# Sums of the first four steps' up weights by accumulating transfers, and the turned input's differences on VectorE

## The chip, the cores and the metric

The kernel runs on one core of a Trainium2 chip. A core has five engines that run beside each other, each with its own queue in program order: TensorE (PE, matrix products), VectorE (DVE), ScalarE (ACT), GpSimd (POOL), and SyncE (SP), which here only issues transfers. Transfers between HBM and the on-chip memory run on 16 DMA engines. The metric is the device time of one execution in microseconds (us); the median of several runs is compared.

## The reference, cut to what matters

The reference is one decoder block over 1024 tokens of width 1024. Its last part is the one that matters here, with 5632 hidden columns of which one half is a value and the other a gate:

```python
def conv_ffn(x, w_up, conv_w, conv_b, w_down):
    h = x @ w_up
    h = causal_depthwise_conv(h, conv_w) + conv_b      # width 3
    a, g = jnp.split(h, 2, axis=-1)
    return (jax.nn.silu(g) * a) @ w_down

h = h + mix @ w_out
h = h + conv_ffn(rmsnorm(h, norm_ffn_g), w_up, conv_w, conv_b, w_down)
return rmsnorm(h, norm_final_g)
```

## The kernel before, in words

**Matrix products.** Float32 operands are taken apart into a high part (a rounded copy, made by ScalarE, L153) and a low part (the rest, by VectorE, L159: `low = source - high`), and three matmuls make one float32 product: high by high, high by low, low by high. So VectorE has one instruction of 128x512 for every weight block. Large products use Winograd's form of the two-by-two block product: seven block products in place of eight, with sums of weight blocks (S1 to S4) and sums of input blocks (T1 to T4) as operands. One block product here is 12 matmuls of 128x512 (function `product`, L1015).

**The passage around the change.** After the eight attention heads the output projection runs over eight blocks of 128 tokens in the order 0, 4, 1, 5, 2, 3, 6, 7 (`wmm`, `hadd`, `norm2`). Each block's result is normed and turned by eight transposes on TensorE (`flip`, L957). For the upper four token blocks `flip` also forms the differences of the turned input: VectorE computes `b11 - p`, `t3`, `t2` (L977 to L979), the high and low parts of T2 and T3 follow (L951, L954), and GpSimd computes `b21 = t2 - b21` (L982). When the last block (7) is turned, `late_sum` (L1044) makes the parts of T1, T4 and B22.

**The up stage** has 22 steps, i = 0 to 21, one for each pair of 128 value columns and 128 gate columns. Step i needs four weight blocks A11, A12 (one load of 512 KB, `upw_a`, L882) and A21, A22 (another, `upw_b`, L898), and the four sums

S1 = A21 + A22, S2 = S1 + A11, S3 = A21 + A11, S4 = S2 + A12,

which GpSimd adds (L907 to L910) into four tiles "sg" of 128x512, a ring of four. In step 1 alone (`inplace`, L902 to L904 and L910) three of the sums are written over the raw blocks, since the ring is taken by step 0. Weights of steps 0 and 1 (AHEAD = 2) are loaded and summed during the last head and the projection; those of step i + 1, from step 2 on, during step i (`nxt_of`, L1141, a generator that `up_b` advances at four places). Raw blocks lie in a ring of four 512 KB tiles "raw"; the parts of A11 and A12 in a ring of four ("wha"), those of S1, S2, S3, S4 and A22 in one of six ("whb"). `product` runs in the order A11, S2, S3, A12, S1, A22, S4 within a step, with the next step's first matmuls drawn ahead.

`up_b` (L1075) puts together the results in VectorE's instructions L1082 to L1105, runs the convolution (L1069 on ScalarE, L1070 and L1072 on VectorE) for gate and value, Silu on ScalarE, and stores the hidden columns and their sums (L1119 to L1124). One order is written out by hand: the low parts of A11 and A12 of steps 2 and 3 stand on VectorE's queue behind the lower gate half of the step before (`gates["hg"]`, L1094). The rest of the order on each queue is a scheduler's; the tile pools put the waits in.

Of the kernel before, what the change touches and what calls it, by code (L numbers as in the profile page):

```python
# [12 lines left out]
ALU = mybir.AluOpType  # L13
# [51 lines left out]
def block_kernel(ctx: ExitStack, tc: tile.TileContext, xT, xtok, wuv, wv, wqk, wf, cpk, bfv,  # L65
                 ggain, g2r, gfr, wsp, woa, wos, wup, wdn, out):
    nc = tc.nc
    act, dve, pool, pe, sp = Line(nc.scalar, tc), Line(nc.vector, tc), Line(nc.gpsimd, tc), nc.tensor, nc.sync
# [22 lines left out]
    def sb(tag, shape, dt=F32):  # L91
        return (raws if tag == "raw" else late if tag in LATE else early).tile(shape, dt, tag=tag, bufs=BUFS[tag], name=nm(tag))
# [7 lines left out]
    def sbank():  # L100
        return psa.tile([P, 512], F32, tag="s", name=nm("ps"))
# [48 lines left out]
    def split_w(src, hl, hi_eng="act", lo_eng="dve"):  # L150
        h, l = hl
        if hi_eng == "act":
            act.copy(h, src)  # L153
        elif hi_eng == "pool":
            pool.tensor_copy(h, src)
        else:
            dve.tensor_copy(h, src)
        eng = dve if lo_eng == "dve" else pool
        return eng.tensor_tensor(out=l, in0=src, in1=f32(h), op=ALU.subtract)  # L159
# [3 lines left out]
    def behind(inst, key):  # L163

        if key in gates:
            after(tc, inst, gates[key])
# [30 lines left out]
    def ring(dt=F32R):  # L197
        rn[0] += 1
        return sb(RTAG[(rn[0] - 1) % 6], [P, 2, 512], dt)
# [10 lines left out]
    def hl_of(n, j, src):  # L210
        act.copy(x2(n, 0, j), src)
        dve.tensor_tensor(out=x2(n, 1, j), in0=src, in1=f32(x2(n, 0, j)), op=ALU.subtract)
# [19 lines left out]
    for p_ in range(2):  # L232
        t = sb("G", [P, 2, 2, 512])
# [100 lines left out]
    for j in range(2):  # L334
        t1, t2, t3 = tmp[j]
# [29 lines left out]
    for j in range(2):  # L365
        t2 = tmp[j][1]
# [66 lines left out]
    W = [Weights(0)]  # L433
# [177 lines left out]
    for k in range(4):  # L611
        t = sb("raw", [P, 2, 512])
# [9 lines left out]
    for hf in (1, 0):  # L622
        for c in range(4):
            src = vgt[hf][:, :, c * P:(c + 1) * P].rearrange("p t (g d) -> p g t d", g=2)
# [17 lines left out]
    for p_ in range(2):  # L642
        t = ring(F32)
# [228 lines left out]
    def ut_(pool_, tag, shape, dt, bufs):  # L872
        return pool_.tile(shape, dt, tag=tag, bufs=bufs, name=nm(tag))
# [3 lines left out]
    AHEAD = 2  # L877
# [13 lines left out]

        return out, split

    def upw_b(i, out, inplace=False):

        a11, a12 = out["ra"][:, 0, :], out["ra"][:, 1, :]
        wr = sb("raw", [P, 2, 512])
        sp.dma_start(out=wr, in_=wup[i, :, 0:2, :])  # L898
        a21, a22 = wr[:, 0, :], wr[:, 1, :]
        if inplace:  # L900
            s = [a21, ut_(upl, "sg", [P, 512], F32, 4), a11, a12]
            pool.tensor_tensor(out=a11, in0=a21, in1=a11, op=ALU.add)  # L902
            pool.tensor_tensor(out=s[1], in0=a11, in1=a22, op=ALU.add)
            pool.tensor_tensor(out=a21, in0=a21, in1=a22, op=ALU.add)  # L904
        else:
            s = [ut_(upl, "sg", [P, 512], F32, 4) for _ in range(4)]
            pool.tensor_tensor(out=s[0], in0=a21, in1=a22, op=ALU.add)  # L907
            pool.tensor_tensor(out=s[1], in0=s[0], in1=a11, op=ALU.add)  # L908
            pool.tensor_tensor(out=s[2], in0=a21, in1=a11, op=ALU.add)
        pool.tensor_tensor(out=s[3], in0=s[1], in1=a12, op=ALU.add)  # L910
        src = {"A22": a22, "S1": s[0], "S2": s[1], "S3": s[2], "S4": s[3]}

        def split(names):
            for n in names:
                t = ut_(upr, "whb", [P, 2, 512], F32R, 6)
                behind(split_w(src[n], (t[:, 0], t[:, 1])), "sums")
                out[n] = t
            return out

        return split  # L920
# [36 lines left out]
    def flip(tt):  # L957

        c = slice((tt % 4) * P, (tt % 4) * P + P)
        pp = []  # L960
        for kh in range(2):
            ps = sbank()
            for j in range(4):
                k = 4 * kh + j
                pe.transpose(ps[:, j * P:(j + 1) * P], xn[tt][:, k * P:(k + 1) * P], ident)
            pp.append(ps.rearrange("p (k t) -> p k t", k=4))
        if tt < 4:
            for n, p3 in (("B11", pp[0]), ("B21", pp[1])):
                hl_of(n, c, p3)
            for n, p3 in (("B11", pp[0]), ("B21", pp[1])):  # L970
                act.copy(xt[n][:, :, c], p3)
            return
        b11, b21, b22 = (xt[n][:, :, c] for n in ("B11", "B21", "B22"))
        t3 = ut_(xtp, "t3", [P, 4, P], F32, 1)
        t2 = ut_(xtp, "t2", [P, 4, P], F32, 1)
        act.copy(b22, pp[1])
        dve.tensor_tensor(out=b11, in0=b11, in1=pp[0], op=ALU.subtract)  # L977
        dve.tensor_tensor(out=t3, in0=b22, in1=pp[0], op=ALU.subtract)
        d = dve.tensor_tensor(out=t2, in0=b22, in1=b11, op=ALU.add)  # L979
        hl_of("T2", c, t2)  # L980
        hl_of("T3", c, t3)
        pool.tensor_tensor(out=b21, in0=t2, in1=b21, op=ALU.subtract)  # L982
        return d

    WA = [upw_a(i) for i in range(AHEAD)]
    W = [WA[0][1](("A11", "A12"))]
    first = (0, 4, 1, 5)
    banks8 = {(tt, hf): (bank() if hf == 0 else sbank()) for tt in first for hf in range(2)}
    for tt in first:
        for hf in range(2):  # L990
            wmm(tt, hf, banks8[tt, hf], (0, 1, 2))
    W.append(WA[1][1](("A11", "A12")))
    WB = [upw_b(0, W[0]), upw_b(1, W[1], True)]
    prev = None
    for tt in (0, 4, 1, 5, 2, 3, 6, 7):
        hload(tt)
        for hf in range(2):
            if tt in first:
                wmm(tt, hf, banks8[tt, hf], (3,))
                hadd(tt, hf, banks8[tt, hf])  # L1000
            else:
                ps = bank()
                wmm(tt, hf, ps, range(4))
                hadd(tt, hf, ps)
        norm2(tt)
        if prev is not None:
            flip(prev)
        prev = tt
# [20 lines left out]
    for i in range(AHEAD):  # L1029
        for j in range(2):  # L1030
            q = psq("a")
            product(q, W[i]["A11" if j == 0 else "A12"], XB["B11" if j == 0 else "B21"], True, True)
            ahead.append(q)
        if i == 0:

            last = flip(7)
            WB[0](("S2", "S3"))
            gates["sums"] = last

    def late_sum(n, src):  # L1040
        for j in range(2):
            k = slice(2 * j, 2 * j + 2)
            act.copy(XB[n][:, 0, k, :], xt[src][:, k, :])
            dve.tensor_tensor(out=XB[n][:, 1, k, :], in0=xt[src][:, k, :], in1=f32(XB[n][:, 0, k, :]), op=ALU.subtract)  # L1044

    late_sum("T1", "B11")
    WB[0](("S1",))
    late_sum("T4", "B21")
# [81 lines left out]
    def waited(i):  # L1130

        x1 = ut_(pst_[0], "u", [P, 512], F32, 5)
        ha = ut_(pst_[0], "h", [P, 1024], F32, 3)
        act.copy(x1, ahead[2 * i])
        dve.tensor_tensor(out=ha[:, 0:512], in0=ahead[2 * i + 1], in1=x1, op=ALU.add)
        return None, x1, ha

    st = waited(0)
    WB[0](("A22", "S4"))

    def nxt_of(i):  # L1141

        if i + 1 == NFF:
            while True:
                yield None
        if i + 1 < AHEAD:
            w, wb = W[i + 1], WB[i + 1]
            wa = lambda names: None
        else:
            w, wa = upw_a(i + 1)  # L1150
            wb = upw_b(i + 1, w)
            W.append(w)
        yield None
        wa(("A11",))
        wb(("S2",))
        yield waited(i + 1) if i + 1 < AHEAD else up_a(i + 1, w)
        wa(("A12",))
        wb(("S3",))
        yield None
        wb(("S1", "A22", "S4"))  # L1160
        yield None
# [21 lines left out]
    for p_, n in ((upl, "B11"), (upl, "T2"), (upl, "B21"), (upl, "T3"), (upr, "T1"), (upr, "T4"), (upr, "B22")):  # L1183
        t = ut_(p_, "x" + n, [P, 2, 4, 512], F32, 1)
# [37 lines left out]
    def blk(b):  # L1222
        return lambda p_: wd[p_][:, b, :]
# [129 lines left out]
```

## Time and profile before

| | |
|---|---|
| median of 3 runs | 1100.56 us (1096.5 to 1100.8) |
| the profiled execution, its own time | 1103.27 us |
| its span in the trace | 1101.5 us |
| granted TensorE clock, mean | 0.991 |
| TensorE busy | 1073.1 us |
| VectorE busy | 900.0 us |
| ScalarE busy | 572.7 us |
| GpSimd busy | 249.2 us |

Times in the rows are microseconds from the span's start. A row of the timeline has the start, the duration, the engine, the line, the operation and its tiles, how often it follows itself, and in brackets how long the engine was idle before it and which instruction released it. Durations overlap the next instruction's start a little, so the distance between starts is the better price of an instruction in a dense row. Windows give the busy time of each engine in a stretch with the number of instructions, and then the granted clock, the busy share of the DMA engines and their GB/s. The matmuls of the up stage's twenty-two steps lie between 452.0 and 884.8 us.

### The profile page before, as it was taken

Reading aid. Unit: us, or ns where it says so; the run is one execution under the profiler, and the core shown is the slowest. Engines: PE = TensorE matmul, PEld = TensorE weight load, DVE = VectorE, ACT = ScalarE, POOL = GpSimd, SP = SyncE. Lnnn points to the kernel's source line nnn. Section 1 sums busy time; section 2 is a strip of 40 time slices with the busy share of each in tenths; the row PEclk is TensorE's granted clock in tenths of the full one; section 3 lists DMA queues with packets and bytes.
Section 4 is the critical chain, followed back from the end, with each engine's and each line's share of the span. In section 5 each row is a group of like instructions: output and inputs, shape, how many; then the busy total and the mean of one; then the engine's idle time right before and its main releaser. Section 6 shows DMA issues by size and latency. Waiting matters only on the chain.

```text
span 1101.5 us, 14438 instructions
## 1 busy us (share of the span) xinstructions
PE 1073.1 (97%) x5013; PEld 881.8 (80%) x5013; DVE 900.0 (82%) x1355; ACT 572.7 (52%) x991; POOL 249.2 (23%) x205
## 2 busy tenths in 40 slices
PE   9999999999998999988999999999999999999997
PEld 6888787777887888766888888888888888888886
DVE  5985799775678977999798989999998876898774
ACT  6656544454468865653444444444444454454653
POOL 0002243133035331334232423333232000000000
PEclk9999999899999999999999999999999999999999
DMA  9242366846548345113123232313321899433342
GB/s 339 85 153 78 100 169 181 231 140 209 189 133 268 98 144 188 70 67 134 68 105 134 78 114 96 124 68 123 116 96 45 270 330 324 122 97 101 124 137 96
DMA packets 64714, 158.18 MB, mean 144 GB/s; under 512 B 7673, under 2 KB 7937, under 8 KB 64641
## 3 DMA queue, kind: packets, MB, share of 16 engines
q1 hardware_dynamic: 64352, 156.70, 42.5%
q8 instruction: 39, 0.64, 0.2%
q10 hardware_dynamic: 288, 0.56, 0.1%
q14 instruction: 35, 0.28, 0.1%
HBM read 114.95 MB, written 42.27 MB: 143 GB/s over the span
## 4 chain that ended last, share of the span: by engine, by line
PE 67%; DVE 7%; ACT 3%; DMA 2%; issue 2%; POOL 1%; SPq 0%; DVEq 0%; ACTq 0%; POOLq 0%
PE k L1210 18%; PE qd L1020 10%; PE qa L1020 10%; PE qc L1020 9%; PE qb L1020 5%; PE pb L794 2%; PE ps L256 2%; PE pb L784 2%; PE pf L824 1%; PE pf L823 1%; PE pf L825 1%; DVE whb L159 1%; DMA rsd<-t 1%; PE ps L759 1%; PE ps L758 1%
## 5 line engine op out<-in xcount | busy, mean ns | idle before, releaser
L1210 PE MATMUL k<-whb,wha 128*128 128x512 f32 x924 | 209.6, 389 | 0.0
L1210 PEld LDWEIGHTS k<-whb,wha 128*128 128x128 f32 x924 | 173.4, 188 | 36.1
L1020 PE MATMUL qa<-xB,wha 128*128 128x512 f32 x528 | 129.4, 395 | 5.7 <-DVE wha L159 5.7
L1020 PE MATMUL qc<-xT,whb 128*128 128x512 f32 x540 | 130.3, 390 | 1.7 <-DVE xT L951 1.3
L1020 PEld LDWEIGHTS qa<-xB,wha 128*128 128x128 f32 x528 | 100.2, 190 | 27.3 <-DVE wha L159 6.5
L1020 PEld LDWEIGHTS qc<-xT,whb 128*128 128x128 f32 x540 | 101.1, 188 | 23.8 <-DVE xT L951 1.8
L153 ACT CAST wha<-sg 128x512 fp32r<-128x512 f32 x77 | 47.9, 622 | 97.3 <-PE k L1210 87.1
L153 ACT CAST whb<-sg 128x512 fp32r<-128x512 f32 x85 | 52.0, 616 | 70.3 <-PE qc L1020 67.7
L159 DVE TENSOR_TENSOR wha<-sg,wha 128x512 fp32r<-128x512 f32 x77 | 52.9, 689 | 42.5 <-ACT wha L153 42.4
L159 DVE TENSOR_TENSOR whb<-sg,whb 128x512 fp32r<-128x512 f32 x85 | 63.0, 742 | 8.9 <-ACT whb L153 8.7
L1020 PE MATMUL qd<-xB,whb 128*128 128x512 f32 x264 | 64.6, 393 | 0.1
L794 PE MATMUL pb<-pt,V 128*128 128x256 f32 (+1 forms) x320 | 60.1, 301 | 4.6 <-ACT pt L785 4.0
L1020 PE MATMUL qd<-xT,whb 128*128 128x512 f32 x264 | 63.4, 389 | 0.0
L1020 PE MATMUL qb<-xT,whb 128*128 128x512 f32 x252 | 61.0, 389 | 1.0 <-DVE whb L159 1.0
L794 PEld LDWEIGHTS pb<-pt,V 128*128 128x128 f32 x320 | 48.0, 192 | 16.6 <-ACT pt L785 11.4
L785 ACT CAST pt<-pb 128x512 fp32r<-128x512 f32 (+1 forms) x80 | 41.0, 543 | 36.7 <-PE pb L784 36.0
L786 DVE TENSOR_TENSOR pt<-pb,pt 128x512 fp32r<-128x512 f32 (+1 forms) x80 | 48.6, 634 | 13.3 <-ACT pt L785 12.8
L1020 PEld LDWEIGHTS qd<-xB,whb 128*128 128x128 f32 x264 | 50.2, 190 | 11.0 <-issue 0.5
L1020 PEld LDWEIGHTS qd<-xT,whb 128*128 128x128 f32 x264 | 49.6, 188 | 10.3
L908 POOL TENSOR_TENSOR sg<-sg,raw 128x512 f32<-128x512 f32 x21 | 42.8, 2038 | 64.7 <-issue 61.3
L907 POOL TENSOR_TENSOR sg<-raw 128x512 f32<-128x512 f32 x21 | 30.7, 1460 | 112.7 <-DVE whb L159 103.4
L1020 PEld LDWEIGHTS qb<-xT,whb 128*128 128x128 f32 x252 | 47.2, 188 | 11.2 <-DVE whb L159 1.4
(391 smaller groups left out, 2310.8 us busy)
## 6 DMA issues: line engine op xcount, KB each, us to landing
raw<-wup SPq DMA_DIRECT2D x44, 512.0 KB, 3.6
sg<-hx SPq DMA_DIRECT2D x77, 256.0 KB, 3.0
hx<-hs SPq DMA_DIRECT2D x44, 256.0 KB, 2.0
hx<-ca SPq DMA_DIRECT2D x33, 256.0 KB, 2.2
xT<-wdn SPq DMA_DIRECT2D x28, 256.0 KB, 5.3
raw<-wqk SPq DMA_DIRECT2D x8, 512.0 KB, 3.3
qd<-G SPq DMA_DIRECT2D x16, 256.0 KB, 3.3
kd<-G SPq DMA_DIRECT2D x16, 256.0 KB, 3.2
```

The costliest lines, as they stand in the source:

```text
L153: act.copy(h, src)
L159: return eng.tensor_tensor(out=l, in0=src, in1=f32(h), op=ALU.subtract)
L256: pe.matmul(banks[m], xs(n, xi, k)[:, ms], w[:, wi, :], start=(first and k == 0 and c == 0), stop=(k == 3 and c == 2), skip_group_check=True)
L758: pe.matmul(ps[:, 0:e - c], A[:, qs], B[:, c:e], start=True, stop=False)
L784: pe.transpose(ptr[:, c:c + P], tj[jj][:, k * P:(k + 1) * P], ident)
L785: act.copy(pt[:, 0, 0:w], ptr[:, 0:w])
L786: dve.tensor_tensor(out=pt[:, 1, 0:w], in0=ptr[:, 0:w], in1=f32(pt[:, 0, 0:w]), op=ALU.subtract)
L794: pe.matmul(po[:, oo:oo + n], lhs, pt[:, s, o:o + n], start=(k == 0 and s == 0), stop=(s == 1 and half))
L907: pool.tensor_tensor(out=s[0], in0=a21, in1=a22, op=ALU.add)
L908: pool.tensor_tensor(out=s[1], in0=s[0], in1=a11, op=ALU.add)
L1020: pe.matmul(ps, w[:, wi, ks], xb[:, xi, k, :], start=(first and n == 0), stop=(n == 11), skip_group_check=True)
L1210: pe.matmul(banks[bk + m], xh[:, xi, ms], wh[:, wi, :], start=(first and p_ == 0 and n == 0), stop=(p_ == NP - 1 and n == 2), skip_group_c ...
```

## The change

For steps 0 to 3 no sum is made by an engine any more. S2's tile is loaded with A11 (a block of 256 KB, on SP's queue), and adding transfers, issued on GpSimd's queue, add blocks from HBM to it and into the raw blocks: `S2 += A21`, `A21 += A22` (which is S1), `S2 += A22`, `A11 += A21` (S3) and `A12 += S2` (S4). That is five adding transfers of 256 KB for each step, written so that the ones to different tiles alternate. The last two write over A11 and A12, so they come behind the high and low parts of these blocks; for steps 2 and 3 they are issued when S3 is asked for. From step 4 on the sums stay on GpSimd. The four subtractions of L982 move to VectorE.

In the order of the changed program fourteen adding transfers (ten of steps 0 and 1, and the two into S2 of each of steps 2 and 3) stand where GpSimd's additions for step 0 began, and the two into A21 of steps 2 and 3 behind them; the two last ones of step 2 stand ahead of step 4's additions, those of step 3 behind the first three of step 4's. On SP's queue the four loads of 256 KB stand ahead of the first h2d stores; the load of step 2's A11 and A12, which stood there (L882 at 411 us), now stands behind the last h2d store, because its place in the ring comes free later. VectorE has each new subtraction next to the T2 and T3 parts, and the parts of T1 behind those of T2 and T3 of the last block.

```diff
-    def upw_b(i, out, inplace=False):
+    def upw_b(i, out):
 
         a11, a12 = out["ra"][:, 0, :], out["ra"][:, 1, :]
         wr = sb("raw", [P, 2, 512])
         sp.dma_start(out=wr, in_=wup[i, :, 0:2, :])
         a21, a22 = wr[:, 0, :], wr[:, 1, :]
-        if inplace:
+        pend = []
+        if i < 4:
+
+            blk = lambda b: wup[i, :, b, :]
+            add = lambda t, src: pool.dma_start(out=t, in_=src, accum_op=ALU.add)
             s = [a21, ut_(upl, "sg", [P, 512], F32, 4), a11, a12]
-            pool.tensor_tensor(out=a11, in0=a21, in1=a11, op=ALU.add)
-            pool.tensor_tensor(out=s[1], in0=a11, in1=a22, op=ALU.add)
-            pool.tensor_tensor(out=a21, in0=a21, in1=a22, op=ALU.add)
+            sp.dma_start(out=s[1], in_=blk(2))
+            add(s[1], blk(0))
+            add(a21, blk(1))
+            add(s[1], blk(1))
+            pend.append(lambda: (add(a11, blk(0)), add(a12, s[1])))
+            if i < AHEAD:
+                pend.pop()()
         else:
             s = [ut_(upl, "sg", [P, 512], F32, 4) for _ in range(4)]
             pool.tensor_tensor(out=s[0], in0=a21, in1=a22, op=ALU.add)
             pool.tensor_tensor(out=s[1], in0=s[0], in1=a11, op=ALU.add)
             pool.tensor_tensor(out=s[2], in0=a21, in1=a11, op=ALU.add)
-        pool.tensor_tensor(out=s[3], in0=s[1], in1=a12, op=ALU.add)
+            pool.tensor_tensor(out=s[3], in0=s[1], in1=a12, op=ALU.add)
         src = {"A22": a22, "S1": s[0], "S2": s[1], "S3": s[2], "S4": s[3]}
 
         def split(names):
+            if "S3" in names and pend:
+                pend.pop()()
             for n in names:
                 t = ut_(upr, "whb", [P, 2, 512], F32R, 6)
                 behind(split_w(src[n], (t[:, 0], t[:, 1])), "sums")
...
         d = dve.tensor_tensor(out=t2, in0=b22, in1=b11, op=ALU.add)
         hl_of("T2", c, t2)
         hl_of("T3", c, t3)
-        pool.tensor_tensor(out=b21, in0=t2, in1=b21, op=ALU.subtract)
+        dve.tensor_tensor(out=b21, in0=t2, in1=b21, op=ALU.subtract)
         return d
...
-    WB = [upw_b(0, W[0]), upw_b(1, W[1], True)]
+    WB = [upw_b(0, W[0]), upw_b(1, W[1])]
```

The changed file is ten lines longer from `upw_b` on, so that a line after it stands ten further down; the text keeps the numbers of the kernel before.

## The prediction

> **What bounds the kernel now.** I read the page first, then TensorE's waits, then the stretch they lie in, cut into windows, then TensorE, VectorE and GpSimd in order of time there.
>
> ```profile
> span 1101.5 us, 14438 instructions
> PE 1073.1 (97%) x5013; PEld 881.8 (80%) x5013; DVE 900.0 (82%) x1355; ACT 572.7 (52%) x991; POOL 249.2 (23%) x205
> ```
>
> TensorE is the bound, so a change in the work of other engines can return only time in which TensorE stood still or ran slowly. Its waits between 440 and 540 us, the passage from the output projection into the up stage (engine, line and what it waited for: us, times, longest):
>
> ```profile
> PE qa L1020 <- DVE wha L159: 5.7, 2, 3.8
> PE qc L1020 <- DVE xT L951: 1.3, 1, 1.3
> PE qb L1020 <- DVE whb L159: 1.0, 1, 1.0
> PE qc L1020 <- DVE u L1086: 0.4, 1, 0.4
> ```
>
> All four wait for VectorE, together 8.4 us. The windows (us, PE, PEld, DVE, ACT, POOL busy, granted clock) show why:
>
> ```profile
> 463.00:477.00 14.00, 11.70 (x50) 8.86 (x49) 14.00 (x17) 8.17 (x12) 2.23 (x2) 1.00 0.11 37
> ...
> 492.00:505.00 13.00, 11.02 (x47) 8.48 (x46) 11.13 (x13) 5.80 (x8) 6.59 (x4) 1.00 0.29 101
> 505.00:520.00 15.00, 11.25 (x48) 9.04 (x47) 15.00 (x19) 4.61 (x7) 7.31 (x3) 0.94 0.38 140
> 520.00:530.00 10.00, 10.00 (x34) 7.95 (x34) 7.60 (x8) 4.56 (x6) 3.49 (x2) 0.74 0.30 107
> 540.00:560.00 20.00, 20.00 (x90) 16.57 (x89) 18.33 (x21) 9.07 (x13) 6.43 (x4) 1.00 0.30 111
> ```
>
> VectorE is full where TensorE has holes; from 540 us on TensorE is full and VectorE has room. After the last hole the granted clock is 0.74. In order of time on TensorE:
>
> ```profile
> 465.60 5.51 PE L1020 MATMUL qc<-xT,whb 128*128 128x512 f32 x23 [1.33 <-DVE xT L951]
> 489.19 3.00 PE L1020 MATMUL qc<-xT,whb 128*128 128x512 f32 x12 [0.35 <-DVE u L1086]
> 496.00 2.60 PE L1020 MATMUL qa<-xB,wha 128*128 128x512 f32 x10 [1.90 <-DVE wha L159]
> 519.12 4.63 PE L1020 MATMUL qa<-xB,wha 128*128 128x512 f32 x10 [3.75 <-DVE wha L159]
> 561.45 2.72 PE qd L1020 x12
> ```
>
> The last row (from the chain of waits, undisturbed) gives one product: 2.72 us for twelve matmuls, 0.227 each, 19.0 for a step of seven products. Ten matmuls should take 2.27; at 519.12 they took 4.63, so the hole of 3.75 is followed by some 2.4 us of slow clock. The most that can come back here is 8.4 + 2.4 = 10.8 us.
>
> Why is VectorE full? Its instructions beside GpSimd's:
>
> ```profile
> 458.54 1.28 DVE L159 TENSOR_TENSOR whb<-sg,whb 128x512 fp32r<-128x512 f32 x2
> 494.79 2.85 DVE L159 TENSOR_TENSOR wha<-raw,wha 128x512 fp32r<-128x512 f32 x2
> 495.36 1.73 POOL L909 TENSOR_TENSOR sg<-raw,raw 128x512 f32<-128x512 f32 x1
> 463.78 2.36 DVE L951 TENSOR_TENSOR xT<-t,xT 128x512 fp32r<-128x512 f32 x2
> 462.73 2.27 POOL L982 TENSOR_TENSOR xtB<-t,xtB 128x512 f32<-128x512 f32 x1
> 461.54 2.32 DVE L1044 TENSOR_TENSOR xT<-xtB,xT 128x1024 fp32r<-128x1024 f32 x1
> 467.81 2.35 DVE L1044 TENSOR_TENSOR xT<-xtB,xT 128x1024 fp32r<-128x1024 f32 x2
> ```
>
> Two low parts of 128x512 take 1.28 us when GpSimd rests (0.60 each, back to back, with 0.08 of overlap) and 2.85 or 2.36 when it adds; one of 128x1024 takes 2.32 beside GpSimd and 2.35 for two without it. So each GpSimd addition costs VectorE about as long as one of its own instructions.
>
> **The change, part by part.** *Removed:* GpSimd's sixteen additions for steps 0 to 3 and its four subtractions of L982. *Added:* four loads of 256 KB on SP's queue, twenty adding transfers of 256 KB on GpSimd's, four subtractions on VectorE. From the instruction order of the changed kernel:
>
> (a) Subtractions on VectorE: 4 x 0.60 = 2.4 us. Two lie before 445 us, where TensorE is fed; two stand in the chain below and are counted there.
>
> (b) Sums of steps 0 and 1, and S2 of steps 2 and 3:
>
> ```profile
> 390.94 1.28 POOL L907 TENSOR_TENSOR sg<-raw 128x512 f32<-128x512 f32 x1 [1.44 <-DMA raw<-wup]
> 409.85 2.50 DVE L159 TENSOR_TENSOR wha<-raw,wha 128x512 fp32r<-128x512 f32 x4 [0.69 <-ACT wha L153]
> 456.06 1.66 ACT L153 CAST whb<-sg 128x512 fp32r<-128x512 f32 x3
> ```
>
> The raw blocks are there at 391 us, the last low part that must come out before its place is added into ends at 412.4, and the longest chain of one step is three adding transfers. Even at 8 us each they are done by 440; their first reader is ScalarE's cast at 456. I cost them at nothing; the work of the projection in between hides them, and if that cover of 16 us were used up, VectorE's whole list from (c) on would move later one for one. The four loads stand in SP's queue behind the first three hpd loads and ahead of the h2d stores; what they delay there would reach VectorE's additions of the projection, and I have no row for how much of it VectorE's waits for TensorE absorb (see the end).
>
> (c) Steps 0 and 1, VectorE's list.
>
> ```profile
> 457.52 1.04 PE L965 MATMUL ps<-ident,xn 128*128 128x128 f32 x8
> ```
>
> T2's last low part now stands before the L1044 parts: these last transposes let VectorE begin at 458.3, and from there it is seventh (L977, a low part, L978, L979, a low part, the new subtraction, T2), 7 x 0.60, so 462.5, ahead of TensorE, which is there at 464 (the wait in the row at 465.60 begins at 464.27, after one matmul); the hole of 1.33 goes. Thereafter thirteen entries (seven of 0.60, six L1044 of 1.13) end at 473.5, where TensorE needs the low part of step 1's S2: 0.2 of 0.97 stays. Nine products from 463.9 on then end at 463.9 + 9 x 2.72 + 0.2 = 488.6 (before: 489.19 + 2.72 = 491.9). The low part of step 2's A11 is held behind the hidden half of step 1 (gate "hg", L1094), which waits for that product: 488.8, then 2 x 0.60 with VectorE not late, 0.2 for the handovers: **490.2, and TensorE restarts on it at 490.3 instead of 496.00**, 5.7 us earlier.
>
> (d) Steps 2 and 3, the new wait. S3 is now added into A11's own place, so it can start only when A11's low part is out, and VectorE's next entries are A12's low part, two convolution passes (0.6 + 2.4 = 3.0 us), and then the low part of S3, in order. Call a the time from the end of A11's low part until the addition has landed. VectorE stands from 3.0 until a + 0.7 (ScalarE's cast), and behind it are the convolution of the value half, the low parts of S1, A22 and S4 and everything to step 3's A11: seventeen entries of 0.60 (10.2), three passes (1.20 + 1.20 + 1.13), about 1.0 of waits for ScalarE. In that stretch step 4's GpSimd additions remain:
>
> ```profile
> 514.44 1.76 DVE L159 TENSOR_TENSOR whb<-raw,whb 128x512 fp32r<-128x512 f32 x1
> 516.13 1.74 DVE L159 TENSOR_TENSOR wha<-raw,wha 128x512 fp32r<-128x512 f32 x1
> 513.33 1.19 DVE L1122 TENSOR_TENSOR hs<-hs,ca 128x512 f32<-128x512 f32 x1
> 509.94 4.03 POOL L907 TENSOR_TENSOR sg<-raw 128x512 f32<-128x512 f32 x1 [7.55 <-DVE whb L159]
> 514.04 1.61 POOL L908 TENSOR_TENSOR sg<-sg,raw 128x512 f32<-128x512 f32 x1
> 515.62 1.70 POOL L909 TENSOR_TENSOR sg<-raw,raw 128x512 f32<-128x512 f32 x1
> ```
>
> They cost VectorE 0.5 + 1.1 + 1.1 = 2.7 here, and I keep that. So from A11 of step 2 to A11 of step 3: a + 0.7 + 10.2 + 3.5 + 1.0 + 2.7 = a + 18.1 us. Before, TensorE's restarts on the two stand at 496.00 and 519.12, 23.1 apart. At a = 5.0 both are equal.
>
> What is a? The trace has no adding transfer and none issued by GpSimd. Nearest rows (KB each, us to landing, the x11 row between 380 and 530 us; ns min/median/max):
>
> ```profile
> sg<-hx SPq DMA_DIRECT2D x77, 256.0 KB, 3.0
> raw<-wup SPq DMA_DIRECT2D x44, 512.0 KB, 3.6
> x<-kd SPq DMA_DIRECT2D x16, 256.0 KB, 8.0
> raw<-wup SPq DMA_DIRECT2D x11, 512.0 KB, 4.3
> L882 SPq DMA_DIRECT2D raw<-wup x22: 327/332/538, 335.4 to 809.2; - x22
> L908 POOL TENSOR_TENSOR sg<-sg,raw x21: 1302/2156/2167, 394.8 to 839.5; 128x512 f32<-128x512 f32 x21
> ```
>
> Landing lies between 3.0 (256 KB) and 8.0 (the slowest 256 KB group); since an addition also reads its target, I take the median of twice the bytes, 3.6. The issue lies between SP's 0.33 and a hindered GpSimd instruction's 2.16; I take the unhindered 1.3. That makes **a about 5.0, bounds 3.3 and 10.2**. The Trainium skill ("DMA: Bandwidth & Descriptors", Anatomy of one DMA — SWDGE (gpsimd) path) has a fit of 2.0 us plus bytes over 436 KB per us for a plain one, 2.6 us here; with the 1.3 that would be a = 3.9, and the sum 1.1 us lower; no run here shows it.
>
> At a = 5.0 TensorE restarts on step 3's A11 at 513.4 instead of 519.12. It ran dry at 490.3 + 19.0 = 509.3; a hole of 4.0 us is like the 3.75 of before, so I keep the slow clock after it. Step 3's S3: GpSimd must first finish step 4's three additions, which wait for a load behind S4's low part (490.2 + a + 0.7 + 6.4 = 502.3, load 4.3, additions 7.3: 513.9), so it is issued at 513.9 and split by 513.9 + a + 1.3 = 520.2. TensorE needs it 31 matmuls after 513.4: at 522.8 with the slow clock as before. No loss until a = 7.5. From step 4 on all is as before.
>
> **Sum:** -5.7 us, and for other a: -5.7 + (a - 5.0) + what a exceeds 7.5 by. The profiled execution took 1103.27 (span 1101.5 and 1.8 around it): 1097.6. It lay 2.7 above the median of the runs shown, so against 1100.56: **1094.9 us**.
>
> **The rivals.** (1) *The additions are quick* (a 3.3 to 4): the step 3 hole shrinks below 3 us and the clock may hold, as it did after the hole of 1.90 (the ten matmuls at 496.00 took 2.60 with overlap). Then -5.7 - 1.4 - 2.4 = -9.5: 1091. For it: the 3.0 row; against: a second read. (2) *The issue is held up by VectorE.* The row at 509.94 shows a GpSimd instruction of 1.28 stretched to 4.03 beside a busy VectorE, and S3's addition is issued just when VectorE has 3.0 us of dense work. If GpSimd gets through only behind that, a = 3.0 + 4.9 = 7.9 and the sum is -5.7 + 2.9 + 0.4 = -2.4: 1098. Against it: that instruction reads and writes whole tiles, an issue does not. The Trainium skill warns of this: in "SBUF — State Buffer", SBUF: two separate sides, GpSimd cannot write a transfer's descriptors while VectorE holds the shared port; in Who interferes with whom it infers that tensor_tensor leaves that write interface free, by which the sum above would stand. No row here shows either. (3) *Transfers that land slowly and only eat the gain* (a 7 to 9): -3.7 to -0.2, 1097 to 1100. (4) *Slower than before:* S3 of steps 2 and 3 is late for TensorE itself, twice. The sum turns positive at 2a = 18.2, a = 9.1, from where each microsecond of a costs two; at a = 13 it is -5.7 + 8.0 + 5.5 = +7.8, 1108. For it: 256 KB already took 8.0 us in one group, GpSimd's share is unseen, and the adding transfers share the 16 engines with 512 KB loads; against: the landing of loads here is 3 to 4. (5) *It does not do what it says:* transfers issued by GpSimd hold VectorE up as its additions did. Then the 5.7 of (c) is gone, 1.2 of subtractions are left, and each of two steps has the wait of a + 0.7 - 3.0 = 2.7: +6.6, 1107. Against it: the long VectorE rows pair with instructions that read SBUF.
>
> **How the numbers follow.** Forecast case (a 4 to 7, 1093.5 to 1097.5) 0.46; quick 0.17; held-up issue 0.08; slow landing 0.06; slower 0.17; not relieved 0.06. A measurement of this kernel can tell about 0.5%, 5.5 us, from no change. The forecast lies at that edge: its lower half counts as faster (0.25 with 0.17 gives 0.42), the other half (0.21) with (2) and (3) as the same (0.35); slower 0.23. The range reaches from the quick case less a microsecond, 1089, to the middle of the slower cases, 1107; the forecast's own is 1092 to 1098.
>
> **What would show it.** Right: VectorE's pairs of low parts between 455 and 500 us back at 1.3; no hole before 480; step 2's A11 with a hole below 0.5; a VectorE wait of a - 2.3 ahead of S3's low part in steps 2 and 3, put down to ScalarE's cast or the transfer; a hole of about 4 us before step 3's A11 and the low clock behind it. Wrong: rows of GpSimd's transfers landing in over 7 us; TensorE waiting on S3's cast; VectorE pairs still at 2.4 beside GpSimd's issues; or holes in the projection before 452 us from crowded transfers.

## The result and the profile after

The changed kernel takes 1101.23 us (median of 20 runs, 1099.13 to 1106.4) against 1098.44 for the kernel before (20 runs, 1096.42 to 1101.91). The ratio is 1.0027 with a 95% interval of 1.0017 to 1.0037, that is 3.0 us slower by the ratio (1.9 to 4.1), where 5.7 us faster was forecast. By the prediction's bound of half a per cent this is "no change", but its sign is clear, and some nine microseconds lie between the forecast and the result.

The profiled execution of the changed kernel took 1100.05 us, span 1098.3. The head of its page and TensorE's waits between 400 and 600 us (engine, line and what it waited for: us, times, longest):

```profile
span 1098.3 us, 14463 instructions
PE 1068.6 (97%) x5013; PEld 878.5 (80%) x5013; DVE 890.9 (81%) x1359; ACT 572.8 (52%) x991; POOL 228.6 (21%) x205
```

```profile
PE ps L975 <- DVE xn L957: 4.6, 1, 4.6
PE qa L1030 <- DVE wha L159: 4.0, 1, 4.0
PE qc L1030 <- DVE u L1096: 1.1, 1, 1.1
PE qd L1030 <- DVE u L1092: 0.4, 1, 0.4
```

VectorE has lost 9 us of work and GpSimd 21, as intended, and of the holes of before only the one ahead of step 3's A11 is left, with 4.0 us (the 0.4 stands in another place). But there are two new ones: 4.6 us at a set of transposes in the projection, and 1.1 in step 5.

The two spans (1101.5 and 1098.3) can't be compared directly. The granted clock dips in some executions ahead of the passage: before had 0.94 in its window of 150 to 200 us and 0.97 in that of 350 to 400, after had 1.00 in both. So I count from the first transposes of the projection. TensorE's rows there, of before and of after:

```profile
424.20 1.09 PE L965 MATMUL ps<-ident,xn 128*128 128x128 f32 x8
```

```profile
419.50 1.09 PE L975 MATMUL ps<-ident,xn 128*128 128x128 f32 x8
431.09 1.85 PE L975 MATMUL ps<-ident,xn 128*128 128x128 f32 x8 [4.62 <-DVE xn L957]
458.74 1.03 PE L975 MATMUL ps<-ident,xn 128*128 128x128 f32 x8
492.36 2.60 PE L1030 MATMUL qa<-xB,wha 128*128 128x512 f32 x10
515.69 3.94 PE L1030 MATMUL qa<-xB,wha 128*128 128x512 f32 x10 [3.95 <-DVE wha L159]
571.74 3.02 PE L1030 MATMUL qc<-xT,whb 128*128 128x512 f32 x12 [1.14 <-DVE u L1096]
```

With the prediction's rows of before, and with one more trace of each kernel (before2 and after2 below), each stretch is:

| stretch, us | before | after | difference |
|---|---|---|---|
| first to last transposes | 33.3, 33.3 | 39.2, 39.3 | +5.9 |
| last transposes to step 2's A11 | 38.5, 38.4 | 33.6, 33.2 | -5.0 |
| step 2's A11 to step 3's A11 | 23.1, 23.3 | 23.3, 23.0 | 0 |
| step 3's A11 to the end | 582.4, 581.3 | 582.6, 583.2 | +1.1 |

The gain that the prediction worked out (5.7) is there as 5.0 us in the second row. The first row takes it away: the hole of 4.6 us itself, and the slow clock behind it (granted 0.52 from 431.1 to 434 us). The +1.1 of the last row is no more than the two traces of before differ by. The sum, 2.0, lies at the lower end of the interval of the medians (1.9 to 4.1).

What happens in the projection is seen in one window of each trace, from 402 to 436 us (busy time of PE, PEld, DVE, ACT, POOL, then granted clock, busy share of the 16 DMA engines, GB/s), before and after:

```profile
402.00:436.00 34.00, 34.00 (x170) 27.96 (x169) 23.92 (x38) 17.09 (x33) 4.58 (x3) 1.00 0.53 187
```

```profile
402.00:436.00 34.00, 29.38 (x134) 23.88 (x133) 20.60 (x34) 15.10 (x29) 10.43 (x12) 0.95 1.02 256
```

The DMA engines go from half busy to full, and TensorE loses 4.6 us. The link is in VectorE's waits and in the DMA issues of after (KB each, us to landing, 398 to 438 us):

```profile
DVE pt L949 <- DMA pt<-hpd: 4.9, 1, 4.9
```

```profile
pt<-hpd SPq DMA_DIRECT2D x6, 512.0 KB, 8.0
sg<-wup POOLq DMA_DIRECT2D x8, 256.0 KB, 6.5
sg<-wup SPq DMA_DIRECT2D x4, 256.0 KB, 7.0
```

"pt<-hpd" is `hload`: each block of the projection loads 512 KB that VectorE adds to TensorE's result (`hadd`) before the norm and the transposes. Its ring has three places, so the fourth load waits until the first block is normed and stored, and VectorE needs it soon after. In before, that distance can be read:

```profile
424.21 6.92 SPq L935 DMA_DIRECT2D pt<-hpd  x3
```

```profile
428.13 0.68 DVE L939 TENSOR_TENSOR pt<-pb,pt 128x512 f32<-128x512 f32 x1
```

Issued at 424.21, used at 428.13: the load had 3.9 us, and VectorE did not wait for it. In after it took 8.0. In the trace of paced2 (below), with most of the new transfers out of its way, it takes 3.4, so its slack is about half a microsecond.

### The profile page after: what moved, and what is told of

Its sections match the earlier page's. It is cut to its first block, busy times and chain, and to the rows that moved or that the text cites. A ratio compares the mean times of both kernels' runs of the same rounds, so it can differ in the third digit from the quotient of the medians.

```text
span 1098.3 us, 14463 instructions
## 1 busy us (share of the span) xinstructions
PE 1068.6 (97%) x5013; PEld 878.5 (80%) x5013; DVE 890.9 (81%) x1359; ACT 572.8 (52%) x991; POOL 228.6 (21%) x205
## 4 chain that ended last, share of the span: by engine, by line
PE 65%; DVE 7%; DMA 5%; ACT 3%; issue 2%; POOL 1%; SPq 0%; DVEq 0%; ACTq 0%; POOLq 0%
PE k L1220 19%; PE qc L1030 9%; PE qd L1030 9%; PE qa L1030 9%; PE qb L1030 5%; PE pb L794 2%; PE ps L256 2%; PE pb L784 2%; PE pf L824 1%; PE pf L823 1%; PE pf L825 1%; DMA raw<-woa 1%; PE ps L759 1%; PE ps L758 1%; DMA raw<-wup 1%
## 5 line engine op out<-in xcount | busy, mean ns | idle before, releaser
L153 ACT CAST whb<-sg 128x512 fp32r<-128x512 f32 x76 | 46.7, 617 | 62.6 <-PE qc L1030 61.0
L159 DVE TENSOR_TENSOR whb<-sg,whb 128x512 fp32r<-128x512 f32 x76 | 56.7, 747 | 9.2 <-ACT whb L153 9.1
L1030 PEld LDWEIGHTS qb<-xT,whb 128*128 128x128 f32 x252 | 47.2, 188 | 10.1 <-DVE whb L159 0.3
L916 POOL TENSOR_TENSOR sg<-sg,raw 128x512 f32<-128x512 f32 x18 | 37.4, 2079 | 58.5 <-issue 57.7
L1080 DVE SCALAR_TENSOR_TENSOR cg<-h,cp,cg 128x1023 f32<-128x1023 f32 x22 | 36.9, 1675 | 14.8 <-ACT cg L1079 14.8
```

The lines of the kernel that those rows point to most:

```text
L1030: pe.matmul(ps, w[:, wi, ks], xb[:, xi, k, :], start=(first and n == 0), stop=(n == 11), skip_group_check=True)
L1080: dve.scalar_tensor_tensor(out=c[:, 1:1024], in0=h[:, 0:1023], scalar=w[1], in1=c[:, 1:1024], op0=ALU.mult, op1=ALU.add)
```

## The experiments

Theory: the fourteen adding transfers (two issued at 387 and 390 us, the others from 406 to 431) and four loads that lie in the projection fill the DMA engines, and the fourth hpd load, which has almost no slack, lands 4 to 5 us late. Rivals: the loss is the wait for S3 on VectorE's queue in steps 2 and 3, and the hole in the projection is an accident of one execution; or the relief of VectorE is worth little. In the diffs, lines are those of the changed kernel unless said otherwise. Ratios are to the kernel before, run on the same chip.

**after2** and **before2**: the two kernels once more, for second traces.

> The changed kernel once more, for a second trace. Crowding theory: a hole of 3.5 to 5.5 us ahead of the third set of transposes and the DMA engines full from 402 to 430 us, as in the first. Rival (an accident of one execution): the hole is below 2 us or elsewhere.

> The kernel before once more, for a second trace. If its first trace is typical: the same four holes of 1.3, 1.0, 1.9 and 3.8 us, no hole over 0.5 in the projection, 677 us from the first transposes to the end; where the clock is an accident of one execution, that stretch differs by up to 3 us with the same holes.

The holes of after2 and of before2 on TensorE:

```profile
433.35 1.94 PE L975 MATMUL ps<-ident,xn 128*128 128x128 f32 x8 [4.01 <-DVE xn L957]
517.86 4.63 PE L1030 MATMUL qa<-xB,wha 128*128 128x512 f32 x10 [3.66 <-DVE wha L159]
574.51 3.01 PE L1030 MATMUL qc<-xT,whb 128*128 128x512 f32 x12 [0.82 <-DVE u L1096]
```

```profile
463.62 5.51 PE L1020 MATMUL qc<-xT,whb 128*128 128x512 f32 x23 [1.36 <-DVE xT L951]
473.50 0.73 PE L1020 MATMUL qb<-xT,whb 128*128 128x512 f32 x2 [0.98 <-DVE whb L159]
493.96 4.15 PE L1020 MATMUL qa<-xB,wha 128*128 128x512 f32 x10 [1.89 <-DVE wha L159]
517.29 3.97 PE L1020 MATMUL qa<-xB,wha 128*128 128x512 f32 x10 [2.38 <-DVE wha L159]
```

Both times the same holes in the same places: no accident. In before2 the last hole is 2.38 instead of 3.75, because ten matmuls ahead of it (493.96) ran with the slow clock (4.15 us instead of 2.60; the granted clock was 0.57 from 494 to 498 us, and 1.00 from 496 to 500 in the first trace) and shortened the wait; the start of step 3's A11 hardly moves (95.1 us after the first transposes, 94.9 in the first trace). A hole's size alone misleads; the distance between starts is steadier.

**crowd**: the kernel before with transfers that do nothing but take DMA time.

```diff
-        pool.tensor_tensor(out=s[3], in0=s[1], in1=a12, op=ALU.add)
+        d = pool.tensor_tensor(out=s[3], in0=s[1], in1=a12, op=ALU.add)
+        if i == 0:
+            for j in range(14):
+                after(tc, pool.dma_start(out=junk[j], in_=wup[j, :, 0:2, :]), d)
```

> The kernel before with 14 transfers of 512 KB from the weights to a scratch block in HBM, issued on GpSimd's queue behind the sums of step 0, so in the projection (about as much DMA engine time as the change's adding transfers; GpSimd's later additions come behind the issues). Crowding theory: the fourth hpd load lands in 7 us or more, a hole of 3 to 6 us ahead of the third set of transposes, total 4 to 8 us slower than before. Rival (the projection does not wait for its loads): within 1 us of before.

1108.46 us, ratio 1.0092 (1.0071 to 1.0112): 10.1 us slower. VectorE waited 8.7 us for the same load, and TensorE:

```profile
436.72 1.94 PE L969 MATMUL ps<-ident,xn 128*128 128x128 f32 x8 [8.42 <-DVE xn L951]
```

Crowding alone, without any adding transfer or new wait in the up stage, makes the hole. It is larger than I expected (3 to 6); the DMA engines stay full up to 430 us here, and the load is also issued 3.5 us after the first transposes, because SyncE waits for the store that frees its place (4.7 us).

**nosum01**: what the relief is worth. It leaves out the sums of steps 0 and 1 (raw blocks stand in their place); those of steps 2 and 3 are GpSimd's again, and the subtraction is VectorE's.

```diff
-        if i < 4:
+        if i < 2:
...
-            s = [a21, ut_(upl, "sg", [P, 512], F32, 4), a11, a12]
-            sp.dma_start(out=s[1], in_=blk(2))
-            add(s[1], blk(0))
...
+            s = [a21, a22, a11, a12]
```

> Leaves out the sums of steps 0 and 1 altogether (raw blocks in their place); those of steps 2 and 3 are GpSimd's as before, the subtraction is VectorE's. No adding transfer at all: what the relief of VectorE is worth without its price. Crowding theory: no hole in the projection, step 2's A11 5 to 6 us earlier after the first transposes than before, total 4 to 8 us faster than before. Rival (the relief itself is worth little): within 2 us of before.

1097.0 us, ratio 0.9976 (0.9960 to 0.9991): 2.6 us faster, no hole in the projection, step 2's A11 at 67.8 us after the first transposes (71.8 in before, so 4.0 earlier). The relief is real, but the gain is below what I expected (5 to 6 us in the trace, 4 to 8 in the time). Its DMA engines from 402 to 436 us are as in before:

```profile
402.00:436.00 34.00, 34.00 (x167) 27.83 (x166) 23.81 (x39) 17.26 (x33) 0.00 (x0) 1.00 0.49 170
```

**adds01** and **late23**: twelve transfers in the projection instead of eighteen. In adds01 the sums of steps 2 and 3 are GpSimd's (`if i < 2`); in late23 their loads and their additions into S2 and A21 (`d` in the diff) are put behind the turning of the last block.

```diff
+            if i >= AHEAD:
+                for x in d:
+                    after(tc, x, turned[0])
```

> Adding transfers for steps 0 and 1 only; the sums of steps 2 and 3 are GpSimd's again, so 12 transfers of 256 KB lie in the projection instead of 18. Crowding theory (the adding transfers fill the DMA engines during the projection, the fourth hpd load takes 8 us and TensorE stands for 4.6): with two thirds of the transfers the hole before the third set of transposes shrinks to 0 to 2.5 us, the gain between 452 and 496 us stays at about 5, and the kernel is 2 to 5 us faster than the one before. Rival (the loss is the wait for S3 in steps 2 and 3 on VectorE's queue, the hole in the projection is an accident of one execution): the hole may stay at any size, VectorE has no wait ahead of S3's low part, the hole of 1.1 us in step 5 goes, 3 to 5 us faster. The two differ in where the trace has its holes.

> As the change, but the loads and the additions into S2 and A21 of steps 2 and 3 stand behind the turning of the last block, so 12 transfers of 256 KB lie in the projection and the waits for S3 in steps 2 and 3 stay. Crowding theory: hole in the projection 0 to 2.5 us, total 0 to 4 us faster than before. Rival (waits for S3): no better than the change, 1 to 4 us slower than before, and the holes of steps 3 and 5 as in the change (4.0 and 1.1 us).

adds01: 1100.04 us, 1.0010 (0.9995 to 1.0025). late23: 1099.1 us, 1.0000 (0.9984 to 1.0016). The holes in the projection, adds01 and late23:

```profile
432.09 1.94 PE L975 MATMUL ps<-ident,xn 128*128 128x128 f32 x8 [2.61 <-DVE xn L957]
```

```profile
432.05 1.06 PE L979 MATMUL ps<-ident,xn 128*128 128x128 f32 x8 [1.37 <-DVE xn L961]
570.08 3.04 PE L1034 MATMUL qc<-xT,whb 128*128 128x512 f32 x12 [0.85 <-DVE u L1101]
```

With fewer transfers the hole shrinks, as the theory says. The two have the same transfers in the projection, and differ by 1.2 us there and by 0.9 in the clock behind it (eight transposes in 1.94 and 1.06): from first to last transposes they take 37.1 and 34.3 us, before 33.3. A single trace can be trusted to about that, and no further. Both holes shrank about as forecast (0 to 2.5), but adds01 missed its forecast of 2 to 5 us faster, and late23 is at the slow end of its own (0 to 4). From step 2's A11 to the end the three hardly differ: 605.8 us with GpSimd's additions (adds01), 605.4 with the adding transfers and their waits (late23), 605.5 and 604.6 in the two traces of before. So in steps 2 and 3 the one price replaces the other, and the rival that puts the loss there falls. late23 keeps the hole in step 5 (0.85), which adds01 doesn't have.

**plain**: the change with `accum_op=ALU.add` taken off: same transfers and waits, the sums left out.

> The change with all its transfers and waits, but the twenty write over their targets instead of adding to them (the sums are left out). If the adding itself takes DMA engine time (a second read): the DMA engines are less than full from 402 to 436 us, the hole in the projection falls from 4.6 to 0 to 2.5 us, total 2 to 5 us less than the change. If the number of transfers and bytes from HBM does it: hole 3.5 to 5.5 and the time of the change within 1.5 us. The wait for S3's low part in step 2 shrinks from 1.4 us if an addition lands later than a copy.

1100.14 us, 1.0010 (0.9994 to 1.0025). TensorE's hole, the window, and GpSimd's DMA queue between 380 and 530 us (packets, MB, share of 16 engines), then that queue's row of the change:

```profile
434.50 0.87 PE L975 MATMUL ps<-ident,xn 128*128 128x128 f32 x3 [3.13 <-DVE xn L957]
```

```profile
402.00:436.00 34.00, 30.87 (x151) 25.31 (x151) 20.55 (x32) 14.40 (x27) 6.44 (x12) 0.97 0.79 270
```

```profile
q0 software_dynamic: 1600, 5.24, 10.9%
```

```profile
q0 software_dynamic: 2880, 5.24, 20.3%
```

Between my two cases: the hole is 3.1, and the time is 1.0010 of before where the change has 1.0027. An adding transfer of 256 KB costs 0.203 x 150 / 20 = 1.52 us of all sixteen engines in 144 packets, a plain one 0.82 us in 80. So adding nearly doubles the price, but eighteen plain transfers at that place already cost most of the hole. VectorE's wait for S3 in step 2 shrinks from 1.4 to 1.0 us, about what the shorter issue saves (0.54 us for 0.86, below).

**sub**: the kernel before with only L982 on VectorE.

> The kernel before with only the subtraction of L982 on VectorE. Prediction's step (c): the hole of 1.33 us on T2's low part goes or shrinks to 0.4, the other holes stay, total 0.5 to 1.5 us faster than before. Rival (VectorE is full and 0.6 us per subtraction comes on top): the hole moves to another instruction, total 0 to 1.5 us slower.

1097.58 us, 0.9992 (0.9978 to 1.0007): 0.9 us faster, not clear of no change. In its trace the hole on T2's low part is 0.62 instead of 1.33, and step 2's A11 comes 69.95 us after the first transposes (71.8 in before). The other holes did not stay as expected: the 0.97 gave way to one of 0.67 beside it, and the 1.90 ahead of step 2's A11 shrank to 0.73. The subtraction is part of the gain in this trace, and a loss from it is not seen.

**paced** and **paced2**: the transfers moved out of the way of the hpd loads, with the waits for S3 kept. paced is late23 with step 1's load and four of its additions behind the last hpd load; paced2 moves three of step 0's additions and its load as well, behind the sixth of the eight hpd loads, and issues the additions into A11 of both steps early (the diff; `gate` is an `hadd` of block 2 for step 0, of block 3 for step 1).

```diff
+            else:
+                early_ = add(a11, blk(0))
+                def rest(gate):
+                    after(tc, sp.dma_start(out=s[1], in_=blk(2)), gate)
+                    after(tc, add(s[1], blk(0)), early_)
+                    add(s[1], blk(1))
+                    add(a12, s[1])
```

> As late23, and of step 1 the load into S2 and four of the five additions stand behind the projection's last hpd load (the fifth, into A21, is early as before): 5 additions and one load of step 0 and one addition of step 1 are left ahead of the fourth hpd load. Crowding theory: that load lands in 3.5 to 5 us, the hole ahead of the third set of transposes is below 0.7 (1.4 in late23, 4.6 in the change), total 1 to 4 us faster than before. Rival (step 1's transfers are now late for TensorE): a hole of over 1 us on step 1's S2 or S3 near 475 us, no faster than late23.

> As paced, and of step 0 too the load into S2, the two additions into it and that into A12 stand behind the projection's hpd loads; ahead of the fourth hpd load only the four additions into A21 and A11 of steps 0 and 1 are left, issued by 412 us. Crowding theory: the DMA engines are idle part of the time between 410 and 420 us, the fourth hpd load lands in under 4.5 us as in the kernel before, no hole over 0.5 us ahead of the third set of transposes (1.49 in paced), total 2 to 5 us faster than before. Rival (S2 of step 0 is late): a hole of over 1 us on S2 or S3 near 462 us and no faster than paced.

paced: 1096.4 us, 0.9980 (0.9965 to 0.9994). paced2: 1095.86 us, 0.9963 (0.9948 to 0.9977). The hole of paced in the projection with its holes in steps 4 and 5, and the window of paced2:

```profile
428.42 1.06 PE L989 MATMUL ps<-ident,xn 128*128 128x128 f32 x8 [1.49 <-DVE xn L971]
545.37 3.02 PE L1046 MATMUL qc<-xT,whb 128*128 128x512 f32 x12 [0.70 <-DVE u L1113]
565.82 3.06 PE L1046 MATMUL qc<-xT,whb 128*128 128x512 f32 x12 [1.12 <-DVE u L1113]
```

```profile
402.00:436.00 34.00, 34.00 (x166) 27.96 (x165) 25.25 (x41) 17.28 (x33) 2.62 (x3) 1.00 0.63 202
```

paced missed its bound on the hole (1.49 for 0.7): three of step 0's additions, issued between 412 and 418 us, were enough. With those out of the way as well the load lands in 3.4 us, and TensorE is never short between 402 and 436 us. All twenty adding transfers are still there, so it was their place that made the hole. The load's landing and the hole go together where the trace has both: 3.4 us and no hole (paced2), 7.3 and 3.1 (plain), 8.2 and 4.0 (after2), 8.0 and 4.6 (the change, where it was issued 0.8 later). In time paced2 is not clear of paced (the intervals overlap). A hole of 1.21 us in step 1 is new in it; it is not that of its rival, which would stand on S2 or S3 near 462 us.

**owns3**: paced with S3 of steps 2 and 3 in its own tile, so that S3's addition no longer waits for A11's low part.

```diff
+                s[2] = ut_(upl, "sg", [P, 512], F32, 4)
...
+                d = [sp.dma_start(out=s[1], in_=blk(2)), sp.dma_start(out=s[2], in_=blk(2)),
+                     add(s[1], blk(0)), add(s[2], blk(0)), add(s[1], blk(1))]
-                pend.append(lambda: (add(a11, blk(0)), add(a12, s[1])))
+                pend.append(lambda: add(a12, s[1]))
```

> As paced, with S3 of steps 2 and 3 in a tile of its own, loaded with A11 and added to ahead of time, so VectorE doesn't wait for A11's low part, the issue and the landing. If the waits for S3 (1.4 and 2.3 us on VectorE in the change) are what VectorE is behind by in steps 4 and 5: the holes of 0.70 and 1.12 there go, the hole ahead of step 3's A11 falls from 3.22 to below 2.2, 1 to 3 us faster than paced. Rival (the convolution and GpSimd's additions of step 4 set VectorE's pace there): holes within 0.5 us of those of paced, total within 1 us of it.

1095.22 us, 0.9958 (0.9943 to 0.9973): 2.4 us less than paced by the ratios (0.9980), but the two intervals overlap a little. VectorE's waits for casts into "whb" between 485 and 530 us, in paced and in owns3, and TensorE's holes of owns3 in step 3:

```profile
DVE whb L159 <- ACT whb L153: 3.6, 4, 1.9
```

```profile
DVE whb L159 <- ACT whb L153: 0.9, 2, 0.6
```

```profile
511.45 1.39 PE L1048 MATMUL qd<-xB,whb 128*128 128x512 f32 x5 [1.05 <-DVE h L1121]
514.36 2.56 PE L1048 MATMUL qa<-xB,wha 128*128 128x512 f32 x10 [1.52 <-DVE wha L159]
```

The holes of 0.70 and 1.12 us that paced has in steps 4 and 5 are gone, and step 3's A11 comes 21.7 us after step 2's (22.6 in paced, 23.1 in before). So the hole in step 5 is the wait for S3, carried on by a VectorE that is 90% busy (45.0 of the 50 us from 520 to 570 in the change) and had no room to catch up in two steps. adds01, without that wait, has no hole in step 5 either.

**both**: paced2 and owns3 together, all sums of steps 0 to 3 still made by adding transfers.

> paced2 and owns3 together: the loads and additions into S2 and A12 of steps 0 and 1 behind the hpd loads, and S3 of steps 2 and 3 in a tile of its own. If the two losses are separate (crowding in the projection, S3 behind A11's low part): no hole over 0.5 us in the projection, holes of step 3 no more than in owns3 (1.05 and 1.52), none in step 5, and 4 to 6 us faster than before. If they feed on each other (S2 of step 0 late, as the hole of 1.21 us in paced2 hints): a hole of about 1.2 us in step 1 stays, and no faster than owns3.

1092.38 us, 0.9946 (0.9927 to 0.9965): 5.9 us faster than before, and the lowest ratio of all, though its interval overlaps that of owns3 and it ran on another chip, beside its own before. No hole in the projection, 1.07 and 1.52 in step 3, none in step 5. The hole of 1.2 us in step 1 stays, as the second case said; ahead of it VectorE waits 1.86 us for a cast:

```profile
485.18 2.97 PE L1043 MATMUL qc<-xT,whb 128*128 128x512 f32 x12 [1.20 <-DVE u L1110]
476.02 1.14 ACT L153 CAST wha<-raw 128x512 fp32r<-128x512 f32 x2 [5.29 <-DMA raw<-wup]
```

That cast stands on ScalarE's queue behind the casts of step 2's A11 and A12 (second row), and these wait 5.29 us for a load that was issued at 469.06. So the late one is a load once more, beside moved transfers, rather than a sum of step 1; no run tests this.

## Why the prediction was wrong

- **Step (b) failed**: "I cost them at nothing; the work of the projection in between hides them." The sums were in time (the last addition issued there landed at 438 us), but the projection around them took 5.9 us longer, more than the whole gain. I asked when the sums are first read (456 us) and found room; I didn't ask what else reads and writes through the same sixteen engines in that time and how much slack it has. The answer stood in the trace of before: an hpd load issued at 424.21 whose user starts at 428.13. The sentence "I have no row for how much of it VectorE's waits for TensorE absorb" points at the place, but only at what the four loads delay on SP's queue, and gave it no price. SP's order was not the point: the fourth hpd load was issued 0.8 us after the first transposes (0.0 in before, and in after2, which has the hole too) and took 8.0 us where 3.9 were to spare.
- **Step (c) was right**: 5.7 us forecast from the last transposes to step 2's A11, 5.0 measured; from the last transposes to 480 us no hole over 0.4, and step 2's A11 with none.
- **Step (d), a**: forecast 5.0 (3.3 to 10.2). The rows of after, on VectorE, GpSimd and ScalarE:

```profile
491.63 1.28 DVE L159 TENSOR_TENSOR wha<-raw,wha 128x512 fp32r<-128x512 f32 x2
497.05 0.69 DVE L159 TENSOR_TENSOR whb<-raw,whb 128x512 fp32r<-128x512 f32 x1 [1.37 <-ACT whb L153]
521.33 0.69 DVE L159 TENSOR_TENSOR whb<-raw,whb 128x512 fp32r<-128x512 f32 x1 [2.32 <-ACT whb L153]
```

```profile
492.71 0.86 POOL L904 DMA_DIRECT2D raw<-wup  x1 [5.34 <-DVE wha L159]
```

```profile
496.40 0.62 ACT L153 CAST whb<-raw 128x512 fp32r<-128x512 f32 x1 [0.81 <-DMA raw<-wup]
```

  A11's low part ends at 492.2, S3 has landed at 496.4: a = 4.2 in step 2, and 5.1 in step 3 (515.6 to 520.7). By the estimate from the Trainium skill's fit ("DMA: Bandwidth & Descriptors", Anatomy of one DMA — SWDGE (gpsimd) path) a would have been 3.9; the prediction took the fit as one for plain transfers, and plain's S3 landed 3.8 us after the low part in step 2 (495.9 to 499.7, with an issue of 0.54) and 4.8 in step 3. The waits on VectorE (1.4 and 2.3 us) were a little shorter than a - 2.3 says. From A11 to A11 it took 23.3 us where a + 18.1 gives 22.3: VectorE also waited for a store to free a place in the ring of "hs", which neither the working nor the trace of before has (its row between 415 and 530 us):

```profile
DVE hs L1132 <- DMA hx<-hs: 2.2, 1, 2.2
```

  The hole ahead of step 3's A11, forecast at about 4 us, was 3.95.

- **"From step 4 on all is as before" failed**, by a hole of 1.1 us in step 5 (0.8 in after2): part of the two waits was paid for there (owns3).
- **Rivals.** (1) and (3) did not occur: a was 4.2 and 5.1. (2) and (5) fall: VectorE's pairs of low parts are back at 1.28 us (491.63), its pass beside the issues at 492.71 and 493.33 took the usual 1.28, and GpSimd's issues took 0.86 to 1.16 with VectorE dense beside them (0.88 at 425.07, where VectorE was idle). That agrees with what the Trainium skill infers in "SBUF — State Buffer", Who interferes with whom, that tensor_tensor leaves the interface free through which descriptors are written. (4) had the right sign by the wrong mechanism: S3 was never late for TensorE. The hole in the projection stood only among the things that would make the prediction wrong. That the time lies inside the range of 1089 to 1107 us is luck: the cases that its upper part was made of did not happen.

## What to carry to other kernels

An empty queue does not make it free to move work from an engine to transfers. List the transfers already in that stretch, and for each the time between its issue and its first use; the one with the least slack is the first to pay. Here it was a load into a ring of three places, which can't be issued before the first block is done with its place. When such a change comes out even, look for the gain and the loss in different stretches before giving it up; here twenty adding transfers as before, placed behind the loads and with one sum in its own tile, turned a loss of 3.0 us into a gain of 5.9.

## What the runs showed of the hardware

- An adding transfer of 256 KB took 1.52 us of all sixteen DMA engines in 144 packets, a plain one 0.82 in 80; its issue held GpSimd for 0.86 us instead of 0.54, and it landed 3.6 to 5.8 us from its issue in steps 2 and 3 (plain 2.9 to 5.4), and 6.5 (median, those into S2) where the engines were full.
- The slow clock behind a hole isn't decided by the hole's size alone: step 2's first ten matmuls of the kernel before took 2.60 us in one trace and 4.15 in the other, after holes of 1.90 and 1.89, and paced had 2.58 behind a hole of 3.22. In the projection eight transposes took 1.06 us behind holes of 1.37 and 1.49, and 1.85 to 1.94 behind 2.61 and more. What decides it was not tried.
